# The first stage takes v ahead of q and k, and layer 0's output path goes ahead of the exponentials

## The chip, the cores and the metric

The kernel runs on one core of a Trainium2 chip. The metric is the time of one execution on the device, in microseconds (us). The five engines of the core are TensorE (PE, with its weight loads as PEld), VectorE (DVE), ScalarE (ACT), GpSimd (POOL) and SyncE (SP), whose queue starts the large transfers.

## The reference, cut to what matters

A decoder trunk of two layers on 256 positions of width 1024. Layer 0 mixes with differential attention, layer 1 with block attention, which for 256 positions is causal attention with 16 heads. Each mixer is followed by a squared-ReLU MLP of width 4096.

```python
h = x
for i in range(2):
    hn = rmsnorm(h, attn_norm[i])
    m = diff_attention(...) if i == 0 else moba_attention(...)
    h = h + m
    h = h + squared_relu_mlp(rmsnorm(h, mlp_norm[i]), w_ff1[i], w_ff2[i])
return rmsnorm(h, final_norm)

# diff_attention: q, k, v = split(hn @ w_in); two score maps p[0], p[1] per head, 8 heads
lam = exp(sum(lf[0] * lf[1])) - exp(sum(lf[2] * lf[3])) + lam_init
a = p[0] - lam * p[1]
o = rmsnorm(a @ v, subln_w) * (1 - lam_init)     # per head
return o @ w_out
```

## The kernel before

**Precision and weights.** Every weight product is made in three matmuls. A weight tile `raw` is split into `hi`, its rounded value (ScalarE, line 141), and `lo`, the rest (VectorE, line 142), and the activations are split in the same way into a high and a low half. `raw` tiles are loaded in units of 1 MB (128 x 2048 floats). Four `raw` buffers and five pairs `hi`/`lo` rotate, so a load waits until the unit four places earlier is split. The list `units` sets the order of the loads. For layer 0 it is: q and k of head 0, the two halves of v's first 512 columns, q and k of heads 1 to 4, v's second half, the other heads, `w_out`, the MLP.

**The first stage** is `start()` and the first block of `mixer(0)`. It stands under `tc.manual_schedule()`, in which the instructions made inside keep the written order on each engine. TensorE first transposes the identity `WARM` times, then the gains, then x: 16 transposes into seven banks of PSUM, first the eight of the first 128 positions, then those of the others. `x_out` (line 214) writes a slice of x, transposed and scaled by the gain, as a high half (ScalarE) and a low half (VectorE). Between the slices stand the splits of unit 0 and then unit 1, in pieces of 512 columns, two of them with `lo` on GpSimd. Then come the sums of squares of x's second half, `root_r` (1/rms, on GpSimd), head 0's q and k (`qk`, 48 matmuls of 256 columns), the first half of `v` (24 matmuls of 512 columns), the split of unit 2, `scale_r` (which writes R, the row factor of q and k), `qk_out` (head 0's q and k times R), the splits of units 3 and 4 and the second half of `v`.

`load_gains()` and `load_lambda()` stand behind that block. There the planner of the framework sets the order on all engines but TensorE, by priorities and by its own estimate of durations, and it may put an instruction ahead of or between those of the block. `tc.high_priority(offset=n)` moves an instruction n places forward in priority (SOONER = 100); split_until uses a negative one (LATER = 150).

**Behind it** TensorE's order is written out and kept (lines 515 to 598): the matmuls of head h, and between them `scores` (with `soft`: the reductions on VectorE and exponentials on ScalarE), `a2` (transposes of the weights of attention to `aT`), `a3` (the product with v, its norm: squares on ScalarE, `on` on VectorE), `a4` (transposes to `oT`, written by `o_out` on ScalarE and VectorE) and `wo` (the products with `w_out`, three matmuls each).

Of the kernel before, what the change touches and what calls it, by code (L numbers as in the profile page):

```python
# [9 lines left out]
F32 = mybir.dt.float32  # L10
F32R = mybir.dt.float32r
# [13 lines left out]
RING = 2048  # L25
LOOK = 3
PIECE = 1024
WARM = 12
LATER = 150
SOONER = 100  # L30

# [2 lines left out]
def kernel(  # L34
# [45 lines left out]
    for i in range(2):  # L80
        qkv = w_in[i].rearrange("(kc d) c -> d kc c", d=P)
        wo = w_out[i].rearrange("(h e) d -> e h d", e=P)
        f1 = w_ff1[i].rearrange("(kc d) f -> d kc f", d=P)
        f2 = w_ff2[i].rearrange("(f p) d -> p f d", p=P)

        def qk_unit(h):
            U[i, "qk", h] = unit([P, 2, KC, P], [
                ((slice(None), s, slice(a, a + n)), qkv[:, a:a + n, s * D + h * P: s * D + (h + 1) * P])
                for s in range(2) for n in ((KC, 4)[i == 0 and h == 0],) for a in range(0, KC, n)])

        def v_unit(g):
            for a in range(2):
                U[i, "v", g, a] = unit([P, 4, 512], [
                    ((slice(None),), qkv[:, 4 * a:4 * a + 4, 2 * D + g * 512: 2 * D + (g + 1) * 512])])

        qk_unit(0)
        v_unit(0)
        for h in range(1, 5):
            qk_unit(h)
        v_unit(1)  # L100
        for h in range(5, 8):
# [13 lines left out]

        for a in range(2):
            f1_unit(0, a)
        for j in range(1, 8):
            for a in range(2):
                f1_unit(j, a)  # L120
                f2_unit(j - 1, a)
        for a in range(2):
            f2_unit(7, a)
# [8 lines left out]
            nc.sync.dma_start(raw[where], src)  # L132
        d["raw"] = raw

    def split_piece(u, c, n, eng=nc.vector):
# [4 lines left out]
        r, h, l = (d[k].rearrange(letters(d["shape"]))[:, c:c + n] for k in ("raw", "hi", "lo"))  # L140
        nc.scalar.activation(h, r, AF.Copy)  # L141
        eng.tensor_tensor(l, r, h.bitcast(F32), op=ALU.subtract)  # L142

    state = dict(loaded=0, done=0, ahead=0)

# [48 lines left out]

    nlam = const.tile([P, 1], F32, name="nlam")

    def load_lambda():
        both = work.tile([1, 4, HD], F32, tag="on", name="lampr", bufs=3)
        pr, one = both[:, 0:2], both[:, 2:4].rearrange("p a b -> p (a b)")
        sm = const.tile([1, 4], F32, name="lamsm")  # L200
        nc.vector.memset(one, 1.0)
        nc.vector.tensor_tensor(pr, lamt[:, 0::2], lamt[:, 1::2], op=ALU.mult)
        nc.vector.reduce_sum(sm[:, 0:2], pr, axis=mybir.AxisListType.X)
        nc.scalar.activation(sm[:, 2:4], sm[:, 0:2], AF.Exp)
        nc.vector.tensor_tensor(sm[:, 0:1], sm[:, 3:4], sm[:, 2:3], op=ALU.subtract)
        nc.vector.tensor_scalar(sm[:, 0:1], sm[:, 0:1], lam_init, None, op0=ALU.subtract)
        t = ps("tp", "lamps")
        mm(t[:, :1], one, sm[:, 0:1], start=True, stop=True)
        nc.vector.tensor_copy(nlam, t[:, :1])


# [42 lines left out]
        return r  # L254


    def start():
        nc.sync.dma_start(xs[:, 0], x_v[:, 0])
        nc.scalar.dma_start(grow0, attn_norm[0].rearrange("(a b) -> a b", b=P))
        nc.sync.dma_start(xs[:, 1], x_v[:, 1])  # L260
        load_until(4)
        load_small()
        load_until(6)
        warm = const.tile([P, 2], F32, name="warm")
        nc.vector.memset(warm, 0.0)
# [7 lines left out]
        parts = new_parts("x")
        xt = xT[0, "a"] = work.tile([P, KC, 2 * T], F32R, tag="xT", name="xT_0a", bufs=1)
        x_ps = [ps(tag, f"xtp0_{j}", bufs) for j, (tag, bufs) in
                enumerate([("acc", 4)] * 4 + [("tp", 2)] * 2 + [("mm", 2)])]
        x_ps = [t_ps[:, :T] for t_ps in x_ps] + [x_ps[4][:, T:]]
        for t in range(NT):
            for kc in range(KC):
                nc.tensor.transpose(x_ps[kc][:, t * P:(t + 1) * P], xs[:, t, kc * P:(kc + 1) * P], ident)  # L280
        for n in range(2):
            sumsq("x", 0, n, parts)
        for kc in range(KC):
            x_out(xt, kc, x_ps[kc], kc)
            if kc in (0, 3):
                split_piece(0, kc // 3 * 512, 512)
            if kc == 6:
                split_piece(0, 1024, 512, nc.gpsimd)
        split_piece(0, 1536, 512, nc.gpsimd)
        for c in range(0, RING, 512):  # L290
            split_piece(1, c, 512)
        state["done"] = 2
        for n in range(2):
            sumsq("x", 1, n, parts)
        return parts
# [4 lines left out]
    def mixer(i, parts):  # L300
# [14 lines left out]
        def qk(h, s, k0, k1, out=True):  # L315

            hi, lo = need(i, "qk", h)
            if s == 0 and k0 == 0:
# [7 lines left out]
            if s == 1 and k1 == KC and out:  # L326
                qk_out(h)

        def qk_out(h):
            o = work.tile([P, 2 * T], F32, tag="qk", name=f"qk{i}_{h}", bufs=4)  # L330
# [3 lines left out]

        def v(g, a):
            hi, lo = need(i, "v", g, a)
            if a == 0:
                S["vp", g] = [ps("acc", f"v{i}_{g}_{t}", 4) for t in range(NT)]
            for t in range(NT):
                o = S["vp", g][t]  # L340
                for c in range(4):
                    kc = 4 * a + c
                    xh, xl = (xt[:, kc, b + t * P: b + (t + 1) * P] for b in (0, T))
                    mm(o, xh, hi[:, c], start=kc == 0, stop=False)  # L344
                    mm(o, xh, lo[:, c], start=False, stop=False)  # L345
                    mm(o, xl, hi[:, c], start=False, stop=kc == KC - 1)  # L346
                if a == 1:
                    vs = work.tile([P, 512], F32, tag="vs", name=f"vs{i}_{g}_{t}", bufs=4)
                    nc.scalar.activation(vs, o, AF.Copy, scale=S["r"][:, t:t + 1])
                    S["v", g, t] = vs  # L350
# [109 lines left out]
        def a4(h):  # L460
            if i == 1:
                return
            t_ps = ps("tp", f"ot{i}_{h}")
            for t in range(NT):
                nc.tensor.transpose(t_ps[:, t * P:(t + 1) * P], S["on", h][:, t], ident)
            o_out(h, t_ps[:, :T], gT[:, GS:])

        def wo(n, t, *hs):
            if ("wo", n, t) not in S:
# [329 lines left out]
```

## Time and profile before

| | |
|---|---|
| median of 3 runs | 605.03 us (604.67 to 605.85) |
| the profiled execution | 604.88 us |
| its span, first to last instruction | 603.1 us |
| TensorE busy | 591.5 us (98%) |
| VectorE, ScalarE, GpSimd busy | 379.8, 318.7, 55.1 us |
| granted TensorE clock, mean | 0.996 |
| read from HBM | 102.25 MB |

In the rows below, a timeline row gives the start and the duration in us, the engine, the line, the operation, what is written and read, and the count of instructions that were merged; in brackets stands the idle time of the engine just before and what ended it. Matmuls overlap, so the distance of two starts, not the duration, is what one costs. Line numbers are those of the kernel before.

### The profile page before, as it was taken

The page shows a single profiled execution, that of the slowest core. Times are in us where ns is not written, and L with a number is a line of the kernel's source. Part 1 is how long each engine was busy: PE and PEld are TensorE (multiplying, and loading weights), DVE is VectorE, ACT ScalarE, POOL GpSimd, SP SyncE. Part 2 cuts the span into 40 slices and gives each one's busy share as a digit, 9 for nine tenths or more (in the row PEclk, how much of TensorE's full clock was granted, in tenths as well). Part 3 has the DMA queues.
Part 4 walks back from the last instruction along what each step waited for, and adds up shares of the span by engine and source line. Part 5 has one row for each costly group of instructions (what it writes and reads, how often), then busy time and mean ns, then how long its engine had stood idle before and what let it go on. Part 6 is the DMA issues. An engine that isn't in the chain of part 4 may idle for free.

```text
span 603.1 us, 8781 instructions
## 1 busy us (share of the span) xinstructions
PE 591.5 (98%) x3368; PEld 506.2 (84%) x3368; DVE 379.8 (63%) x704; ACT 318.7 (53%) x614; POOL 55.1 (9%) x82
## 2 busy tenths in 40 slices
PE   7999999999999999999999999999999999999995
PEld 6899897888888888888889988878888888888884
DVE  4798578488466466466566664638776476476534
ACT  5776476375354354354474656637554454454413
POOL 5001011000000000000000661500000000000003
PEclk8999999999999999999999999999999999999999
DMA  9996444166646646646848436533566646645001
GB/s 303 264 329 222 148 132 140 71 210 200 211 148 204 214 141 210 209 140 199 215 145 210 141 139 180 174 102 108 182 203 213 201 143 218 199 140 209 0 1 70
DMA packets 85258, 103.87 MB, mean 172 GB/s; under 512 B 2112, under 2 KB 67936, under 8 KB 85216
## 3 DMA queue, kind: packets, MB, share of 16 engines
q1 hardware_dynamic: 84896, 103.03, 54.8%
q8 instruction: 26, 0.43, 0.3%
q10 hardware_dynamic: 160, 0.27, 0.1%
q14 instruction: 16, 0.13, 0.1%
q0 software_dynamic: 160, 0.01, 0.0%
HBM read 102.25 MB, written 1.05 MB: 171 GB/s over the span
## 4 chain that ended last, share of the span: by engine, by line
PE 92%; DVE 2%; ACT 2%; POOL 1%; DMA 1%; issue 1%; POOLq 0%; DVEq 0%
PE y L644 29%; PE f L620 20%; PE f L621 10%; PE z L323 5%; PE z L324 5%; PE z L325 5%; PE v L345 2%; PE v L346 2%; PE v L344 2%; PE wo L478 2%; PE wo L480 2%; PE wo L479 2%; PE s L363 2%; PE at L410 1%; ACT e L386 1%; PE o L433 1%
## 5 line engine op out<-in xcount | busy, mean ns | idle before, releaser
L142 DVE TENSOR_TENSOR lo<-raw,hi 128x1024 fp32r<-128x1024 f32 (+1 forms) x194 | 232.5, 1211 | 130.4 <-ACT hi L141 130.1
L141 ACT ACTIVATE hi<-raw 128x1024 fp32r<-128x1024 f32 (+1 forms) x196 | 197.5, 1038 | 150.5 <-PE f L620 84.6
L644 PE MATMUL y<-hi,h 128*128 128x512 f32 x504 | 167.7, 396 | 0.0
L644 PEld LDWEIGHTS y<-hi,h 128*128 128x128 f32 x504 | 94.8, 188 | 23.1 <-ACT h L629 0.3
L644 PE MATMUL y<-lo,h 128*128 128x512 f32 x252 | 99.9, 397 | 0.0
L620 PE MATMUL f<-xT_(1, 'm')_4142,hi 128*128 128x512 f32 x256 | 91.9, 397 | 0.0
L620 PE MATMUL f<-xT_(0, 'm')_1443,hi 128*128 128x512 f32 x256 | 91.9, 397 | 0.0
L621 PE MATMUL f<-xT_(1, 'm')_4142,lo 128*128 128x256 f32 x256 | 72.3, 282 | 0.0
L621 PE MATMUL f<-xT_(0, 'm')_1443,lo 128*128 128x256 f32 x256 | 72.3, 282 | 0.0
L620 PEld LDWEIGHTS f<-xT_(0, 'm')_1443,hi 128*128 128x128 f32 x256 | 48.2, 188 | 11.7
L620 PEld LDWEIGHTS f<-xT_(1, 'm')_4142,hi 128*128 128x128 f32 x256 | 48.2, 188 | 11.7
L644 PEld LDWEIGHTS y<-lo,h 128*128 128x128 f32 x252 | 47.4, 188 | 8.9
L629 ACT ACTIVATE h<-zs 128x256 fp32r<-128x256 f32 x64 | 26.0, 410 | 46.2 <-DVE zs L627 46.2
L621 PEld LDWEIGHTS f<-xT_(1, 'm')_4142,lo 128*128 128x128 f32 x256 | 48.1, 188 | 1.2
L621 PEld LDWEIGHTS f<-xT_(0, 'm')_1443,lo 128*128 128x128 f32 x256 | 48.1, 188 | 1.2
L325 PE MATMUL z<-xT_0a,lo 128*128 128x256 f32 x128 | 36.4, 285 | 2.3 <-DVE lo L142 2.3
L323 PE MATMUL z<-xT_0a,hi 128*128 128x256 f32 x128 | 37.6, 293 | 0.0
L323 PE MATMUL z<-xT_(1, 'a')_2915,hi 128*128 128x256 f32 x128 | 36.7, 286 | 0.0
L324 PE MATMUL z<-xT_0a,hi 128*128 128x256 f32 x128 | 36.6, 286 | 0.0
L630 DVE TENSOR_TENSOR h<-zs,h 128x256 fp32r<-128x256 f32 x64 | 27.0, 424 | 15.0 <-ACT h L629 14.5
L625 ACT ACTIVATE zs<-f 128x256 f32<-128x256 f32 x64 | 23.9, 375 | 23.4 <-PE f L621 23.4
L324 PE MATMUL z<-xT_(1, 'a')_2915,hi 128*128 128x256 f32 x128 | 35.9, 280 | 0.0
(190 smaller groups left out, 826.6 us busy)
## 6 DMA issues: line engine op xcount, KB each, us to landing
raw<-in_w_ff_dram SPq DMA_DIRECT2D x64, 1024.0 KB, 5.4
raw<-in_w_in_dram SPq DMA_DIRECT2D x30, 512.0 KB, 5.6
raw<-in_w_in_dram SPq DMA_DIRECT2D x8, 1024.0 KB, 5.1
raw<-in_w_out_dram SPq DMA_DIRECT2D x8, 1024.0 KB, 5.2
xs<-in_x_dram SPq DMA_DIRECT2D x2, 512.0 KB, 3.9
raw<-in_w_in_dram SPq DMA_DIRECT2D x4, 256.0 KB, 5.5
fg<-in_final_norm_dram SPq DMA_DIRECT2D x2, 256.0 KB, 3.9
out_dram<-xg SPq DMA_DIRECT2D x2, 256.0 KB, 2.0
```

Source lines behind the costliest of these rows:

```text
L141: nc.scalar.activation(h, r, AF.Copy)
L142: eng.tensor_tensor(l, r, h.bitcast(F32), op=ALU.subtract)
L323: mm(z, hi[:, s, kc], xh, start=s == 0 and kc == 0, stop=False, skip_group_check=True)
L324: mm(z, hi[:, s, kc], xl, start=False, stop=False, skip_group_check=True)
L325: mm(z, lo[:, s, kc], xh, start=False, stop=s == 1 and kc == KC - 1, skip_group_check=True)
L344: mm(o, xh, hi[:, c], start=kc == 0, stop=False)
L620: mm(z, hi[:, kc, c], xt[:, kc], start=kc == 0, stop=False, skip_group_check=True)
L621: mm(z[:, :T], lo[:, kc, c], xt[:, kc, :T], start=False, stop=kc == KC - 1, skip_group_check=True)
L625: nc.scalar.activation(zs, z[:, T:], AF.Copy)
L629: nc.scalar.activation(h[:, :T], zs, AF.Copy)
L630: nc.vector.tensor_tensor(h[:, T:], zs, h[:, :T].bitcast(F32), op=ALU.subtract)
L644: mm(acc[n, t], a, w[:, f % 2, n * 512:(n + 1) * 512], start=f == 0 and w is hi and a is hh, skip_group_check=i == 1, stop=a is hl and (f ...
```

## The change

In the first stage v's first half becomes unit 0 and 1, ahead of head 0's q and k (now unit 2). x is loaded in two halves of its columns (all positions each) instead of two halves of its positions, with the first two slices of unit 0 between them. x is transposed two slices at a time into one bank (`x_slice`), and v's matmuls of a slice follow as soon as it is split; slices 4 to 7 follow in pairs, with the split of unit 1 in pieces of 1024 columns. No `lo` goes to GpSimd any more. All four sums of squares stand behind x. `load_gains` and the two parts of the lambda work stand in the written order inside the block. The split of unit 3 (head 1) stands at its end, and unit 4 behind it. Outside the first stage, `a3` of layer 0 and the `o_out` of heads 4 and 5 get SOONER. WARM goes from 12 to 10.

```diff
-WARM = 12
+WARM = 10
 ...
+        if i == 0:
+            v_unit(0)
         qk_unit(0)
-        v_unit(0)
+        if i == 1:
+            v_unit(0)
 ...
-    def load_lambda():
-        both = work.tile([1, 4, HD], F32, tag="on", name="lampr", bufs=3)
 ...
+    def lambda_sums():
+        nc.vector.memset(lam_ab[:, 2:4], 1.0)
+        nc.vector.tensor_tensor(lam_ab[:, 0:2], lamt[:, 0::2], lamt[:, 1::2], op=ALU.mult)
+        nc.vector.reduce_sum(lam_s[:, 0:2], lam_ab[:, 0:2], axis=mybir.AxisListType.X)
+
+    def lambda_out():
+        nc.scalar.activation(lam_s[:, 2:4], lam_s[:, 0:2], AF.Exp)
+        nc.vector.tensor_tensor(lam_s[:, 0:1], lam_s[:, 3:4], lam_s[:, 2:3], op=ALU.subtract)
+        nc.vector.tensor_scalar(lam_s[:, 0:1], lam_s[:, 0:1], lam_init, None, op0=ALU.subtract)
         t = ps("tp", "lamps")
+        mm(t[:, :1], lam_ab[:, 2:4].rearrange("p a b -> p (a b)"), lam_s[:, 0:1], start=True, stop=True)
         nc.vector.tensor_copy(nlam, t[:, :1])
 ...
+    def start_loads():
         nc.scalar.dma_start(grow0, attn_norm[0].rearrange("(a b) -> a b", b=P))
 ...
+        nc.sync.dma_start(xs[:, :, :512], x_v[:, :, :512])
+        for c in range(2):
+            nc.sync.dma_start(u["raw"][:, c:c + 1], src[:, c:c + 1])
+        nc.sync.dma_start(xs[:, :, 512:], x_v[:, :, 512:])
+        nc.sync.dma_start(u["raw"][:, 2:], src[:, 2:])
+        state["loaded"] = 1
+        load_until(6)
         load_small()
-        load_until(6)
 ...
+    def x_slice(g):
+        t_ps = ps("tp", f"xtp0_{g}")
+        for c in range(2):
+            for t in range(NT):
+                nc.tensor.transpose(t_ps[:, c * T + t * P: c * T + (t + 1) * P],
+                                    xs[:, t, (2 * g + c) * P:(2 * g + c + 1) * P], ident)
+        return [t_ps[:, c * T:(c + 1) * T] for c in range(2)]
 ...
         def a3(*hs):
+            with tc.high_priority(offset=SOONER if i == 0 else 0):
+                a3_(*hs)
 ...
-            o_out(h, t_ps[:, :T], gT[:, GS:])
+            with tc.high_priority(offset=SOONER if h in (4, 5) else 0):
+                o_out(h, t_ps[:, :T], gT[:, GS:])
 ...
             with tc.manual_schedule():
-                parts = start()
+                start_loads()
+                start_warm()
+                parts = new_parts("x")
+                xt = xT[0, "a"] = work.tile([P, KC, 2 * T], F32R, tag="xT", name="xT_0a", bufs=1)
+                xp = x_slice(0) + x_slice(1)
+                for kc in range(4):
+                    x_out(xt, kc, xp[kc], kc)
+                    split_piece(0, kc * 512, 512)
+                    v_mm(0, [(t, kc) for t in range(NT)], units[0]["hi"], units[0]["lo"])
+                    if kc >= 2:
+                        xp += x_slice(kc)
+                for kc in range(4, 8, 2):
+                    x_out(xt, kc, xp[kc], kc)
+                    x_out(xt, kc + 1, xp[kc + 1], kc + 1)
+                    split_piece(1, (kc - 4) * 512, 1024)
+                v_mm(0, [(t, kc) for kc in range(4, 8) for t in range(NT)], units[1]["hi"], units[1]["lo"])
+                for n in range(2):
+                    for t in range(NT):
+                        sumsq("x", t, n, parts)
+                lambda_sums()
                 root_r()
-                xt = xT[i, "a"]
-                qk(0, 0, 0, 8, out=False)
-                qk(0, 1, 0, 8, out=False)
-                v(0, 0)
+                state["done"] = 2
                 split_until(3)
+                qk_mm(0, 0, 0, 8, units[2]["hi"], units[2]["lo"])
+                load_gains()
                 scale_r()
+                qk_mm(0, 1, 0, 8, units[2]["hi"], units[2]["lo"])
+                lambda_out()
+                v_out(0)
                 qk_out(0)
-                split_until(5)
-                v(0, 1)
+                split_until(4)
             state["ahead"] = LOOK
-            load_gains()
-            load_lambda()
```

`qk_mm`, `v_mm` and `v_out` are the matmuls of `qk`, those of `v` and the copies at the end of `v` as functions of their own. In `v_mm` the three matmuls of a slice and a half of the positions follow one another: x high with `hi`, x high with `lo`, x low with `hi`.

## Rows read from the trace of the kernel before

**Rows 1.** The page, part 1: busy time, share of the span and count by engine.
```profile
PE 591.5 (98%) x3368; PEld 506.2 (84%) x3368; DVE 379.8 (63%) x704; ACT 318.7 (53%) x614; POOL 55.1 (9%) x82
```
**Rows 2.** Waits of TensorE, whole span: us in total, times, longest.
```profile
PE z L325 <- DVE lo L142: 2.3, 1, 2.3
...
PE wo L478 <- ACT oT L421: 0.9, 1, 0.9
PE at L410 <- DVE on L457: 0.2, 1, 0.2
```
**Rows 3.** Timeline of TensorE, 4.5 to 14.1 us.
```profile
4.50 3.34 PE L280 MATMUL xtp<-ident,xs 128*128 128x128 f32 x16
...
5.19 1.06 PE L280 MATMUL xtp<-ident,xs 128*128 128x128 f32 x4
...
7.11 0.73 PE L280 MATMUL xtp<-ident,xs 128*128 128x128 f32 x4
7.76 0.38 PE L323 MATMUL z<-xT_0a,hi 128*128 128x256 f32 x1
7.99 0.28 PE L324 MATMUL z<-xT_0a,hi 128*128 128x256 f32 x1
10.58 0.44 PE L325 MATMUL z<-xT_0a,lo 128*128 128x256 f32 x1 [2.32 <-DVE lo L142]
...
14.09 0.33 PE L324 MATMUL z<-xT_0a,hi 128*128 128x256 f32 x1
```
**Rows 4.** Timeline of VectorE, first 31 us.
```profile
9.64 0.28 DVE L202 TENSOR_TENSOR lampr<-lamt 1x128 f32<-1x128 f32 x1 [1.94 <-DMA lamt<-in_diff_lambda_dram]
9.85 0.67 DVE L142 TENSOR_TENSOR lo<-raw,hi 128x512 fp32r<-128x512 f32 x1
10.46 1.25 DVE L217 SCALAR_TENSOR_TENSOR xT_0a<-xtp,gT,xT_0a 128x256 fp32r<-128x256 f32 x3
...
24.63 0.69 DVE L332 TENSOR_TENSOR qk<-z,R 128x512 f32<-128x512 f32 x1 [3.57 <-ACT R L313]
25.57 4.63 DVE L142 TENSOR_TENSOR lo<-raw,hi 128x1024 fp32r<-128x1024 f32 x4 [0.26 <-ACT hi L141]
```
**Rows 5.** Windows: stretch, length, busy (instructions) by engine, granted clock, DMA share, GB/s.
```profile
10.75:11.00 0.25, 0.25 (x2) 0.21 (x3) 0.25 (x2) 0.19 (x1) 0.00 (x0) 0.55 1.07 401
14.00:14.25 0.25, 0.25 (x3) 0.25 (x2) 0.25 (x2) 0.25 (x2) 0.00 (x0) 0.63 1.10 342
18.00:23.00 5.00, 5.00 (x23) 4.03 (x22) 2.79 (x6) 1.61 (x2) 0.73 (x1) 1.00 1.21 295
30.00:38.00 8.00, 8.00 (x69) 8.00 (x69) 8.00 (x12) 7.22 (x8) 0.00 (x0) 1.00 1.09 359
```
**Rows 6.** The page, part 6: DMA issues, KB each, us from issue to landing.
```profile
xs<-in_x_dram SPq DMA_DIRECT2D x2, 512.0 KB, 3.9
```
**Rows 7.** Timeline of ScalarE, first 29 us.
```profile
6.72 0.47 ACT L216 ACTIVATE xT_0a<-xtp,gT 128x256 fp32r<-128x256 f32 x1 [1.05 <-PE xtp L280]
7.09 0.62 ACT L141 ACTIVATE hi<-raw 128x512 fp32r<-128x512 f32 x1
...
23.93 0.39 ACT L312 ACTIVATE R<-rps 128x256 f32<-128x256 f32 x1 [4.32 <-PE rps L311]
...
24.48 3.90 ACT L141 ACTIVATE hi<-raw 128x1024 fp32r<-128x1024 f32 x4
```
**Rows 8.** Timeline of TensorE, 97 to 106 us.
```profile
97.68 0.39 PE L465 MATMUL ot<-ident,on 128*128 128x128 f32 x2
...
105.31 0.83 PE L445 MATMUL o<-vs,aT 128*128 128x128 f32 x6
```
**Rows 9.** Timeline of ScalarE, 101 to 105 us.
```profile
101.52 0.82 ACT L421 ACTIVATE oT<-ot,gT 128x256 fp32r<-128x256 f32 x2
102.23 2.00 ACT L141 ACTIVATE hi<-raw 128x1024 fp32r<-128x1024 f32 x2
104.13 0.49 ACT L412 ACTIVATE aT<-at 128x384 f32<-128x384 f32 x1
```

More of the change, by code (lines that the diff above doesn't have):

```diff
@@ L88, in qk_unit @@
                 ((slice(None), s, slice(a, a + n)), qkv[:, a:a + n, s * D + h * P: s * D + (h + 1) * P])
-                for s in range(2) for n in ((KC, 4)[i == 0 and h == 0],) for a in range(0, KC, n)])
+                for s in range(2) for a, n in ((0, KC),)])
         def v_unit(g):
@@ L133, in load, with split_tiles @@
         d["raw"] = raw
-    def split_piece(u, c, n, eng=nc.vector):
+    def split_tiles(u):
         d = units[u]
@@ L139, in split_piece, with split_part @@
             d["lo"] = wsp.tile(d["shape"], F32R, tag="lo", name=f"lo{u}")
-        r, h, l = (d[k].rearrange(letters(d["shape"]))[:, c:c + n] for k in ("raw", "hi", "lo"))
+        return d["raw"], d["hi"], d["lo"]
+    def split_part(r, h, l):
         nc.scalar.activation(h, r, AF.Copy)
-        eng.tensor_tensor(l, r, h.bitcast(F32), op=ALU.subtract)
+        nc.vector.tensor_tensor(l, r, h.bitcast(F32), op=ALU.subtract)
+    def split_piece(u, c, n):
+        split_part(*(k.rearrange(letters(units[u]["shape"]))[:, c:c + n] for k in split_tiles(u)))
     state = dict(loaded=0, done=0, ahead=0)
@@ L195 @@
     nlam = const.tile([P, 1], F32, name="nlam")
-    def load_lambda():
-        both = work.tile([1, 4, HD], F32, tag="on", name="lampr", bufs=3)
[L199 to L206, printed above, removed]
+    lam_ab = work.tile([1, 4, HD], F32, tag="on", name="lampr", bufs=3)
+    lam_s = const.tile([1, 4], F32, name="lamsm")
+    def lambda_sums():
[6 more added lines that the diff above has]
+        nc.vector.tensor_scalar(lam_s[:, 0:1], lam_s[:, 0:1], lam_init, None, op0=ALU.subtract)
         t = ps("tp", "lamps")
-        mm(t[:, :1], one, sm[:, 0:1], start=True, stop=True)
+        mm(t[:, :1], lam_ab[:, 2:4].rearrange("p a b -> p (a b)"), lam_s[:, 0:1], start=True, stop=True)
         nc.vector.tensor_copy(nlam, t[:, :1])
@@ L254, in rsqrt, with start_warm @@
         return r
-    def start():
-        nc.sync.dma_start(xs[:, 0], x_v[:, 0])
+    def start_loads():
         nc.scalar.dma_start(grow0, attn_norm[0].rearrange("(a b) -> a b", b=P))
-        nc.sync.dma_start(xs[:, 1], x_v[:, 1])
-        load_until(4)
+        u = units[0]
+        u["raw"] = wraw.tile(u["shape"], F32, tag="raw", name="raw0")
+        src = u["pieces"][0][1]
+        nc.sync.dma_start(xs[:, :, :512], x_v[:, :, :512])
[5 more added lines that the diff above has]
+        load_until(6)
         load_small()
-        load_until(6)
+    def start_warm():
         warm = const.tile([P, 2], F32, name="warm")
@@ L272, in start @@
         nc.vector.tensor_copy(gT[:, :KC], t_ps[:, P:P + KC])
[L273 to L295, printed above, removed]
+    def x_slice(g):
[5 more added lines that the diff above has]
+        return [t_ps[:, c * T:(c + 1) * T] for c in range(2)]
     slopes8 = [2.0 ** (-8.0 * (h + 1) / 8) for h in range(8)]
@@ L317, in qk, with qk_mm @@
             hi, lo = need(i, "qk", h)
+            qk_mm(h, s, k0, k1, hi, lo)
+            if s == 1 and k1 == KC and out:
+                qk_out(h)
+        def qk_mm(h, s, k0, k1, hi, lo):
             if s == 0 and k0 == 0:
@@ L325, in qk @@
                 mm(z, lo[:, s, kc], xh, start=False, stop=s == 1 and kc == KC - 1, skip_group_check=True)
-            if s == 1 and k1 == KC and out:
-                qk_out(h)
         def qk_out(h):
@@ L336, in v, with v_mm, v_out @@
             hi, lo = need(i, "v", g, a)
-            if a == 0:
-                S["vp", g] = [ps("acc", f"v{i}_{g}_{t}", 4) for t in range(NT)]
-            for t in range(NT):
[L340 to L350, printed above, removed]
+            v_mm(g, [(t, 4 * a + c) for t in range(NT) for c in range(4)], hi, lo)
+            if a == 1:
+                v_out(g)
+        def v_mm(g, tk, hi, lo):
+            if (0, 0) in tk:
+                S["vp", g] = [ps("acc", f"v{i}_{g}_{t}", 4) for t in range(NT)]
+            for t, kc in tk:
+                o = S["vp", g][t]
+                c = kc % 4
+                xh, xl = (xt[:, kc, b + t * P: b + (t + 1) * P] for b in (0, T))
+                mm(o, xh, hi[:, c], start=kc == 0, stop=False)
+                mm(o, xh, lo[:, c], start=False, stop=False)
+                mm(o, xl, hi[:, c], start=False, stop=kc == KC - 1)
+        def v_out(g):
+            for t in range(NT):
+                vs = work.tile([P, 512], F32, tag="vs", name=f"vs{i}_{g}_{t}", bufs=4)
+                nc.scalar.activation(vs, S["vp", g][t], AF.Copy, scale=S["r"][:, t:t + 1])
+                S["v", g, t] = vs
         blocks = ((0, slice(0, P)), (1, slice(P, 384)))
@@ L426, in a3, with a3_ @@
         def a3(*hs):
+            with tc.high_priority(offset=SOONER if i == 0 else 0):
+                a3_(*hs)
+        def a3_(*hs):
             O = {h: ps("tp", f"o{i}_{h}") for h in hs}
```

## The prediction

> **What bounds the kernel now.** I read the page first. TensorE is busy for 591.5 us of a span of 603.1, 98% [rows 1], so the time is the sum of its instructions plus its few waits and whatever stretch runs at the low clock. The waits of TensorE come next. Behind its first instruction it has only three: 2.3 us for a `lo` tile of the weights, 0.9 us for an `oT` tile and 0.2 us for a buffer that `on` frees [rows 2]. So only two places can gain: the first 15 us and the output path of layer 0 near 100 us. The profiled execution took 604.88 us, 1.78 more than its span. The sum below is made against 604.88. The median of the other runs, 605.03, lies 0.15 above it.
>
> The timeline shows the start. Sixteen transposes of x run from 4.50 to 7.76, about 0.21 us apart. Two matmuls on q weights follow, and then nothing starts until 10.58 [rows 3]. VectorE shows why. It stood at a lambda instruction for 1.94 us until the DMA of lambda landed at 9.64, and the `lo` tile that TensorE wanted was queued behind it [rows 4]. The clock comes after that. The granted clock is half (1.2 of 2.4 GHz) from about 10.8 to 14.2, right behind the empty stretch [rows 5]. The granted column shows full speed before that, but the instructions say otherwise. Four transposes took 1.06 us around 5.2 and 0.73 us from 7.11 on [rows 3], so the engine was slow until about 7.2.
>
> **The change, part by part.** *Removed at the start.* From the matmul at 7.99 to the one at 10.58 the list has 2.59 us where 0.12 is normal (69 matmuls in 8 us [rows 5]), so 2.47 goes. From 10.58 to 14.09, 14 matmuls on 256 columns take 3.51 us [rows 3] where 14 x 0.118 = 1.65 would do, so 1.86 goes, if the clock stays up. Lambda now stands behind the sums of squares, and its DMA has long landed by then, so it costs nothing. Eight of the 16 transposes of x move to about 12 us, to full speed: 8 x (0.21 - 0.11) = 0.8. Together 5.1 us.
>
> *Added at the start.* The loads of x by columns move the same bytes. The old halves took 3.9 us to land [rows 6], the first new one stands first on the queue too, and I keep 4.3 for it. The pieces of v behind it, 256 KB each, are due about 0.7 us after one another at the 342 to 401 GB/s of [rows 5], ahead of their use. Two warm-up transposes less end in time that TensorE waits anyway. So only four waits are to be priced.
>
> (a) The first matmul. Eight transposes end at 4.5 + 8 x 0.21 = 6.2. The first bank of four is done at about 5.65. ScalarE then takes 0.37 for `x_out` until the split can start, and 0.62 for the split [rows 7], so the first matmul starts at 6.65. The second needs `lo`, 0.67 more on VectorE [rows 4], and starts at 7.4. TensorE stands for 0.45 + 0.45 = 0.9. Bounds: 0.5, if `x_out` need not wait for the whole bank, and 1.6, if the first transfer lands 0.7 later. After that each slice of x costs VectorE 0.42 + 0.67 = 1.1 and TensorE six matmuls of 0.23 (23 in 5 us [rows 5]) = 1.4, so the vector engines keep ahead for slices 0 to 3.
>
> (b) The second half of v. Slices 4 and 5 are transposed behind slice 2's matmuls. From there the chain is two `x_out`s (0.75), a split of 1024 columns on ScalarE (3.90 / 4 = 0.98 [rows 7], 1.05 for one alone), VectorE's half of it (4.63 / 4 = 1.16 [rows 4]) and 0.2 of hand-overs, about 3.1. TensorE meanwhile has slice 3 (1.4) and four transposes (0.4). It waits 1.25. Bounds 0.6 and 1.7, by how far the engines overlap.
>
> (c) Head 0's weights are split after four sums of squares on ScalarE. By the same durations they arrive 0.2 after TensorE (bounds 0 and 0.6).
>
> (d) Head 1's weights. In the first stage each engine keeps the written order. The trace shows it: ScalarE stood for 4.32 us before R, and the splits behind it, with all their data there, followed only at 24.48 [rows 7]; VectorE did the same before `qk_out` [rows 4]. The change puts the split of head 1 last, behind `lambda_out`, `v_out` and `qk_out`. VectorE can start `qk_out` only when head 0's last matmul and the lambda matmul are through, about 0.45 later. It takes 0.6 to hand over and the `lo` half 1.2, so it is ready 2.3 after the matmuls of head 0. TensorE is at that matmul after 0.55 and waits 1.75. Before, 5.6 us of v matmuls covered this split; now nothing does. Bounds 0.8 (if `qk_out` overlaps further) and 2.4. Behind the waiting matmul stands all of TensorE's list.
>
> Together 0.9 + 1.25 + 0.2 + 1.75 = 4.1.
>
> (e) The clock. It was up at about 7.2, after transposes without a break from 4.50. Now that run ends at 6.2, with two gaps behind it. If it rises at the same time all the same, the cost is 0. If it comes as late behind the first steady matmuls as it did in the slow stretch, 3.4 us [rows 5], it is up at 10.8, and half of 3.4 us is lost: 1.7. The work from 7.4 on is like the work in that stretch, so I take a value nearer that end, 1.2.
>
> The Trainium skill, TensorE: Matmul & The Clock Gate, section Part 4: PE-mode transpose, says that transposes do not raise the clock, since they don't count as busy in the way that matmuls do. This trace disagrees: the transposes sped up before any weight matmul had run [rows 3]. By that rule term (e) would be the full 1.7 and the time half a microsecond more than I forecast; that is rival 4.
>
> Net at the start: -5.1 + 4.1 + 1.2 = +0.2.
>
> *The output path of layer 0.* The transposes of head 4 are done at about 98.1 [rows 8], but ScalarE wrote its `oT` only at 101.52, behind all exponentials of heads 6 and 7 [rows 9]. With the two tiles put 100 places sooner that wait ends: -0.94. The 0.2 us wait for `on` should go with the raised `a3`: -0.19. What is late next: the exponentials move back by the two tiles (0.7), so ScalarE's work up to 102.23 and the two splits behind it end when they did, and `aT` of head 6 is still written at 104.13 [rows 9]. TensorE wants it at 105.31 - 0.94 = 104.37 [rows 8], and it is complete at 104.62: +0.25 (bounds 0, if it comes ahead of a split, and 0.5). Together -0.9 (bounds -1.1 and 0).
>
> Everything after that is TensorE's own list, with no wait in the trace. The splits run later than before: those of head 2 were done at 30.2 [rows 4] and are now due near 32.7, and TensorE comes to them after head 1's 48 matmuls, near 35. That cover is 2 us, and I cost them at 0.
>
> *Sum:* +0.2 - 0.9 = -0.7, so 604.88 - 0.7 = 604.2 for the profiled execution, 604.3 beside the median.
>
> **Rivals.**
> 1. *The clock is up early and the waits overlap more.* For it: the transposes did raise it in the trace, and half as many stand there again. Against it: their run is broken. (e) goes to 0 and (b) or (d) to 0.2 less: 604.3 - 1.4 = 602.9.
> 2. *Slower: the wait before head 1 drops the clock.* TensorE stands still for 1.75 us at about 27 us. The empty 2.3 us of rows 2 were followed by the half clock; the 0.9 us at 102 were not. [...] The price is what the trace shows for such a stretch, 1.86, and where the clock is that easily lost, (e) is at its upper end (0.5 more): 604.3 + 2.4 = 606.7.
> 3. *The output path does not move.* The order outside the first stage is made by the planner, and a raised priority helps only where the planner believes the tile ready. Then the 0.9 stays: 605.2.
> 4. *Transposes don't count for the clock.* Then the clock rises only behind the weight matmuls, at 10.8 (1.7 instead of 1.2): 604.8. The quicker transposes from 7.11 on [rows 3] speak against it.
>
> **How the numbers follow.** The forecast, 604.3, has 0.34 and its own range is 603.6 to 605.2. Rival 1 has 0.32, rival 2 has 0.16, rival 3 has 0.10, rival 4 has 0.08. A change under 0.2%, 1.2 us, can hardly be told from none here. Below 603.8 lie nearly all of rival 1 and a sixth of the forecast: 0.37 for faster. Above 606.2 lie most of rival 2 and a little of rival 3: 0.14. The rest, 0.49, is no change. The range goes from 602.5 (rival 1 with two waits at their lower bounds) to 606.4 (rival 2 with (e) at its middle value).
>
> **What would show it.** The trace after should have no wait for the DMA of lambda. TensorE's first weight matmul should stand near 6.7 and the second near 7.4, with a wait of about 1.2 near 14 us and one of 1.75 before `z` of head 1, near 28 us. The chain from x should be read by the spacing of the v matmuls: 0.43 apart until the clock is up, 0.23 after. The `oT` rows of heads 4 and 5 should stand among the exponentials. I am wrong if `z` of head 1 doesn't wait, if the clock is full from the first v matmul on, or if a wait of over 1 us shows up behind 40 us.

## The result: 7 us slower, half of it at the start and half behind it

The changed kernel takes 611.97 us (611.81 to 614.38), the kernel before 604.93 on the same chip: a ratio of 1.0123 (95% interval 1.0096 to 1.015). I had forecast 604.3, from 602.5 to 606.4. The profiled execution took 611.91 us, 7.03 more than that of before.

First, how much work there is. Part 1 of the page of the changed kernel:

```profile
PE 592.5 (97%) x3366; PEld 504.6 (83%) x3366; DVE 379.9 (62%) x704; ACT 318.7 (52%) x612; POOL 52.5 (9%) x80
```

TensorE is busy 1.0 us longer than in [rows 1], in a span 7.0 us longer. So the loss is nearly all waiting. Two places in the timelines say where it arose: the start of the scores of heads 0 and 1 on TensorE, and the first sum of a `w_out` product on VectorE. Start and duration in us, before:

```profile
38.48 1.58 PE L363 MATMUL s<-qk 64*128 64x128 f32 x16
...
116.73 1.39 DVE L486 TENSOR_TENSOR xs<-wo,xs 128x512 f32<-128x512 f32 x2 [3.93 <-PE wo L480]
```

and after:

```profile
42.22 1.58 PE L375 MATMUL s<-qk 64*128 64x128 f32 x16
...
123.80 1.39 DVE L503 TENSOR_TENSOR xs<-wo,xs 128x512 f32<-128x512 f32 x2 [3.93 <-PE wo L497]
```

The scores start 3.74 us later, where I had forecast +0.2. From the scores to the `w_out` sum (I call it stretch 2) it takes 81.58 us instead of 78.25, that is +3.33, where I had forecast -0.9. Together 7.07. Behind it the two kernels take the same time: 603.1 - 116.73 = 486.4 and 610.1 - 123.80 = 486.3.

The waits of TensorE after (us in total, times, longest):

```profile
PE ot L481 <- DVE oT L434: 4.1, 2, 2.3
PE z L333 <- DVE lo L147: 2.3, 2, 1.5
...
PE xtp L296 <- DMA xs<-in_x_dram: 1.2, 1, 1.2
PE wo L497 <- DVE oT L434: 0.2, 1, 0.2
```

The wait on an `oT` tile of [rows 2] fell from 0.9 to 0.2. The first row is new and the largest, and I had not named it. The timeline of TensorE after, with the idle time before an instruction and what ended it in brackets:

```profile
1.55 2.39 PE L288 MATMUL wps<-ident 128*128 128x128 f32 x10 [1.55 <-POOL ident masks.py:199]
...
5.37 1.97 PE L296 MATMUL xtp<-ident,xs 128*128 128x128 f32 x8 [1.22 <-DMA xs<-in_x_dram]
7.56 0.79 PE L354 MATMUL v<-hi,xT_0a 128*128 128x512 f32 x1 [0.23 <-ACT hi L146]
8.29 0.79 PE L355 MATMUL v<-lo,xT_0a 128*128 128x512 f32 x1
...
11.86 0.40 PE L354 MATMUL v<-hi,xT_0a 128*128 128x512 f32 x1
...
17.09 0.49 PE L354 MATMUL v<-hi,xT_0a 128*128 128x512 f32 x1 [0.70 <-ACT hi L146]
...
18.35 0.50 PE L355 MATMUL v<-lo,xT_0a 128*128 128x512 f32 x1 [0.77 <-DVE lo L147]
...
24.27 0.28 PE L332 MATMUL z<-xT_0a,hi 128*128 128x256 f32 x1
25.28 0.38 PE L333 MATMUL z<-xT_0a,lo 128*128 128x256 f32 x1 [0.74 <-DVE lo L147]
...
31.95 0.28 PE L332 MATMUL z<-xT_0a,hi 128*128 128x256 f32 x1
33.78 0.38 PE L333 MATMUL z<-xT_0a,lo 128*128 128x256 f32 x1 [1.55 <-DVE lo L147]
...
67.30 0.44 PE L481 MATMUL ot<-ident,on 128*128 128x128 f32 x2 [2.29 <-DVE oT L434]
...
95.96 0.44 PE L481 MATMUL ot<-ident,on 128*128 128x128 f32 x2 [1.78 <-DVE oT L434]
```

The forecast waits are there, with one more: two at the first matmuls, two instead of one in v's second half (17.09 and 18.35), one before head 0 (25.28), longer than forecast, and 1.55 before head 1 (33.78). The two at 67.30 and 95.96 stand before the `ot` transposes of heads 1 and 3.

### The profile page after: what moved, and what is told of

Its sections match the earlier page's. It is cut to its first block, busy times and chain, and to the rows that moved or that the text cites. A ratio compares the mean times of both kernels' runs of the same rounds, so it can differ in the third digit from the quotient of the medians.

```text
span 610.1 us, 8769 instructions
## 1 busy us (share of the span) xinstructions
PE 592.5 (97%) x3366; PEld 504.6 (83%) x3366; DVE 379.9 (62%) x704; ACT 318.7 (52%) x612; POOL 52.5 (9%) x80
## 4 chain that ended last, share of the span: by engine, by line
PE 85%; DVE 7%; ACT 3%; DMA 2%; issue 1%; POOL 1%; POOLq 0%; DVEq 0%
PE y L679 28%; PE f L655 20%; PE f L656 10%; PE z L331 3%; DVE lo L147 3%; PE z L333 3%; PE z L332 3%; PE v L354 2%; PE v L355 2%; PE wo L495 2%; PE wo L497 2%; PE v L356 2%; PE wo L496 2%; ACT hi L146 1%; PE s L375 1%
## 5 line engine op out<-in xcount | busy, mean ns | idle before, releaser
L655 PE MATMUL f<-xT_(0, 'm')_1434,hi 128*128 128x512 f32 x256 | 91.9, 397 | 0.0
L655 PE MATMUL f<-xT_(1, 'm')_4133,hi 128*128 128x512 f32 x256 | 91.9, 397 | 0.0
L656 PE MATMUL f<-xT_(1, 'm')_4133,lo 128*128 128x256 f32 x256 | 72.3, 282 | 0.0
L656 PE MATMUL f<-xT_(0, 'm')_1434,lo 128*128 128x256 f32 x256 | 72.3, 282 | 0.0
L655 PEld LDWEIGHTS f<-xT_(1, 'm')_4133,hi 128*128 128x128 f32 x256 | 48.2, 188 | 11.7
L655 PEld LDWEIGHTS f<-xT_(0, 'm')_1434,hi 128*128 128x128 f32 x256 | 48.2, 188 | 11.7
L656 PEld LDWEIGHTS f<-xT_(1, 'm')_4133,lo 128*128 128x128 f32 x256 | 48.1, 188 | 1.2
L656 PEld LDWEIGHTS f<-xT_(0, 'm')_1434,lo 128*128 128x128 f32 x256 | 48.1, 188 | 1.2
L331 PE MATMUL z<-xT_0a,hi 128*128 128x256 f32 x128 | 36.8, 287 | 0.0
L331 PE MATMUL z<-xT_(1, 'a')_2906,hi 128*128 128x256 f32 x128 | 36.7, 286 | 0.0
L332 PE MATMUL z<-xT_(1, 'a')_2906,hi 128*128 128x256 f32 x128 | 35.9, 280 | 0.0
```

Source lines behind the costliest of these rows:

```text
L655: mm(z, hi[:, kc, c], xt[:, kc], start=kc == 0, stop=False, skip_group_check=True)
L656: mm(z[:, :T], lo[:, kc, c], xt[:, kc, :T], start=False, stop=kc == KC - 1, skip_group_check=True)
```

## The experiments

Each ratio is to runs of the kernel before on the same chip; those had medians from 605.26 to 605.69. The time is the median of the runs. "Scores" and "stretch 2" are the two measures from above; they are read from the one profiled execution of each kernel.

| kernel | time | ratio [95%] | scores | stretch 2 |
|---|---|---|---|---|
| before | 604.93 to 605.69 | 1 | 38.48 | 78.25 |
| after | 611.97 | 1.0123 [1.0096, 1.015] | 42.22 | 81.58 |
| a_noprio | 610.06 | 1.0073 [1.0058, 1.0088] | 43.07 | 79.02 |
| a_noa3 | 609.4 | 1.006 [1.0046, 1.0073] | 43.10 | 78.49 |
| a_oout_all | 612.68 | 1.012 [1.0099, 1.0142] | 43.01 | 83.12 |
| b_a3 | 608.53 | 1.0053 [1.0036, 1.0069] | 38.62 | 81.20 |
| b_oout | 604.23 | 0.9982 [0.9973, 0.9991] | 38.56 | 77.66 |
| a_head1 | 609.73 | 1.0067 [1.0052, 1.0082] | 40.97 | 80.51 |
| a_banks | 611.32 | 1.0097 [1.0081, 1.0114] | 39.65 | 83.38 |
| a_warm | 611.83 | 1.0107 [1.0084, 1.013] | 42.53 | 83.11 |
| a_xcols | 612.62 | 1.0119 [1.0101, 1.0137] | 42.94 | 81.56 |
| b_lam | 602.75 | 0.9955 [0.994, 0.997] | 35.92 | 79.01 |
| b_lam_oout | 602.31 | 0.9951 [0.9936, 0.9966] | 35.78 | 77.78 |
| a_fixed | 603.2 | 0.9961 [0.9948, 0.9973] | 37.25 | 77.76 |

**Stretch 2: which of the two priorities?** The theory: the raised `a3` makes the new `ot` waits. The rival: raising only two of the eight `oT` tiles does it. Four kernels, two from either side.

b_a3, the kernel before with only `a3` raised:
```diff
 def a3(*hs):
+    with tc.high_priority(offset=SOONER if i == 0 else 0):
+        a3_(*hs)
```


> The kernel before with a3 of layer 0 raised by 100 places and nothing else. Theory 1: the ot transposes wait twice for about 2 us, in heads 1 and 3, so 604.9 + 4 = about 609. Theory 2: no such wait, 604.7 to 604.9.

Measured 608.53, scores unmoved and stretch 2 longer by 2.95. Its waits of TensorE hold the two of the changed kernel, at the same heads; the first is 1.21 here instead of 2.29, the second 1.78 as there:
```profile
PE ot L469 <- DVE oT L422: 3.0, 2, 1.8
...
PE wo L482 <- ACT oT L421: 0.9, 1, 0.9
```
```profile
62.84 0.44 PE L469 MATMUL ot<-ident,on 128*128 128x128 f32 x2 [1.21 <-DVE oT L422]
```
The `wo` row shows that `a3` alone does not bring `oT` of head 4 forward either.

b_oout, the kernel before with only the `o_out` of heads 4 and 5 raised:
```diff
-            o_out(h, t_ps[:, :T], gT[:, GS:])
+            with tc.high_priority(offset=SOONER if h in (4, 5) else 0):
+                o_out(h, t_ps[:, :T], gT[:, GS:])
```


> The kernel before with o_out of heads 4 and 5 raised and nothing else. Both theories: the 0.9 us wait before wo goes and nothing comes for it, 604.9 - 0.9 = 604.0. If the planner is not moved by it, 604.9.

Measured 604.23. Stretch 2 is 0.59 shorter, and the wait at `wo` is down to 0.2. This half of the output path is a small gain, as forecast.

a_noprio, the changed kernel with neither raised:
```diff
-offset=SOONER if i == 0 else 0
+offset=0
 ...
-offset=SOONER if h in (4, 5) else 0
+offset=0
```


> The changed kernel with both priorities of the output path taken back (a3 and o_out as before), the first stage as changed. Theory 1: the two new waits of the ot transposes (2.3 and 1.8 us) come from the raised a3. Then they vanish, the 0.9 us wait before wo comes back, and the time is 612.0 - 4.1 + 0.9 = 608.8. Theory 2 (rival): they come from the first stage, which ends 3.7 us later and makes the planner choose another order. Then they stay and the time is about 612.9.

Measured 610.06. The `ot` waits are gone and stretch 2 is 79.02. That is still 0.77 above before, by two waits of TensorE for `on` (0.8 together) that before had once with 0.2 [rows 2]. The new one:
```profile
66.17 0.55 PE L422 MATMUL at<-ident,e 128*128 128x128 f32 x3 [0.64 <-DVE on L473]
```
The time is 1.3 above theory 1, by this wait and by scores that came 0.85 later than in the changed kernel (the clock, below).

a_oout_all, the changed kernel with the `oT` tiles of all eight heads raised:
```diff
-offset=SOONER if h in (4, 5) else 0
+offset=SOONER
```


> The changed kernel with o_out of all heads of layer 0 raised, not only of heads 4 and 5. If the new waits of ot come from this, that a3 was raised past the oT of heads 0 and 2, which stayed where they were, they go and the time is 612.0 - 4.1 = 607.9. If raising a3 delays the oT tiles in another way (its squares among the exponentials), they stay at 2 us each: 612.

Measured 612.68. The rival falls: the `ot` waits are still 3.9 us. In the profiled execution, the slowest of the four, TensorE also stood at the half clock behind the first of them (68 to 72 us, below).

a_noa3, the changed kernel with only `a3` not raised:
```diff
-offset=SOONER if i == 0 else 0
+offset=0
```


> The changed kernel with only the raised a3 taken back; o_out of heads 4 and 5 stays raised. Theory: the two waits of ot (4.1 us) are all that the raised a3 brought, and o_out of heads 4 and 5 alone removes the wait before wo: 612.0 - 4.1 + 0.2 (the wait for on comes back) = 608.1, and what is left over the kernel before, 2.7 to 3, is the first stage (3.7) less the output path (0.9). Rival: the raised a3 also helped somewhere (the norms of heads 4 to 7 come sooner), and taking it back gains under 3 us.

Measured 609.4. Stretch 2 is 3.09 shorter than in the changed kernel. The time fell by 2.6 only, because in its profile the scores came 0.9 later (the clock, below).

How the raised `a3` does it stands in the order on VectorE. After, 62 to 67 us:
```profile
62.37 0.15 DVE L470 SCALAR_TENSOR_TENSOR v<-sq,c 128x2 f32<-128x2 f32 x1
...
63.40 0.61 DVE L473 TENSOR_SCALAR on<-o,rs_o 128x128 f32<-128x128 f32 x2 [0.72 <-POOL rs_o L263]
...
64.64 0.68 DVE L338 TENSOR_TENSOR qk<-z,R 128x512 f32<-128x512 f32 x1
...
65.63 1.22 DVE L147 TENSOR_TENSOR lo<-raw,hi 128x1024 fp32r<-128x1024 f32 x1
66.77 0.48 DVE L434 SCALAR_TENSOR_TENSOR oT<-ot,gT,oT 128x256 fp32r<-128x256 f32 x1
```
Before, the same work at 59 to 62 us:
```profile
59.03 0.15 DVE L454 SCALAR_TENSOR_TENSOR v<-sq,c 128x2 f32<-128x2 f32 x1
59.10 0.68 DVE L332 TENSOR_TENSOR qk<-z,R 128x512 f32<-128x512 f32 x1
60.07 0.61 DVE L457 TENSOR_SCALAR on<-o,rs_o 128x128 f32<-128x128 f32 x2 [0.28 <-POOL rs_o L253]
60.60 0.47 DVE L422 SCALAR_TENSOR_TENSOR oT<-ot,gT,oT 128x256 fp32r<-128x256 f32 x1
60.99 1.22 DVE L142 TENSOR_TENSOR lo<-raw,hi 128x1024 fp32r<-128x1024 f32 x1
```
The reader is to see two things. Before, `qk_out` fills the time in which GpSimd works out `rs_o`, and `oT` of head 0 follows `on` directly, ahead of the split. After, `on` was raised, so VectorE comes to it sooner and stands still for 0.72; `qk_out` and a split of 1.22 then come ahead of `oT`. The same order stands at the second wait (`on` at 92.06 after 0.60 of standing, the split at 94.29, `oT` at 95.42). The first of these `oT` frees the bank of PSUM that `ot` of head 1 needs, and TensorE waits 2.29 for it. Without the raise, in a_noa3, the old order is back:
```profile
65.57 0.61 DVE L473 TENSOR_SCALAR on<-o,rs_o 128x128 f32<-128x128 f32 x2 [0.28 <-POOL rs_o L263]
66.09 0.48 DVE L434 SCALAR_TENSOR_TENSOR oT<-ot,gT,oT 128x256 fp32r<-128x256 f32 x1
```

**The start: the wait before head 1.** a_head1, the changed kernel with the split of head 1 directly behind that of head 0, ahead of R, lambda and `qk_out`:
```diff
                 state["done"] = 2
-                split_until(3)
+                split_until(4)
 ...
-                split_until(4)
```


> The changed kernel with head 1's split (unit 3) moved up, directly behind head 0's, ahead of lambda_out, v_out and qk_out. Theory (step d of the prediction): the wait of 1.7 us at the lo matmul of head 1 comes only from that place in the written order, since ScalarE and VectorE stand idle for 3.8 and 2 us before; it goes, and the scores of heads 0 and 1 start 1.6 to 1.8 us sooner than at 42.2. Rival: the data of unit 3 are late too (transfer or splits), and the wait moves by less than half a microsecond.

Measured 609.73; the wait before head 1 is gone:
```profile
PE ot L481 <- DVE oT L434: 3.0, 2, 1.8
...
PE z L333 <- DVE lo L147: 0.8, 1, 0.8
```
The 0.8 left is head 0's. Scores came 1.25 sooner, not 1.6 to 1.8, with a clock that rose later (near 13 us; 11.9 in the changed kernel). Stretch 2 is 1.07 shorter too, since the first `ot` wait is down from 2.29 to the 1.21 of b_a3:
```profile
64.98 0.44 PE L481 MATMUL ot<-ident,on 128*128 128x128 f32 x2 [1.21 <-DVE oT L434]
```
So the late split of head 1 costs a second time, some 30 us behind its own wait. The other changed kernels agree. Those that keep the wait before head 1 have a first `ot` wait of 2.06 to 2.36 or, without the raised `a3`, the new wait for `on` of a_noprio (0.64; 0.66 in a_noa3). a_fixed, without either, has only the 0.2 for `on` of the kernel before. By which steps the late split does this was not followed.

**The start: the shared bank.** In the changed kernel slices 4 and 5 of x lie in one bank. ScalarE's `x_out` of slice 5 stood behind VectorE's of slice 4, though the two slices lie in different halves of it:
```profile
14.59 0.47 ACT L226 ACTIVATE xT_0a<-xtp,gT 128x256 fp32r<-128x256 f32 x1 [3.41 <-PE xtp L296]
15.62 0.47 ACT L226 ACTIVATE xT_0a<-xtp,gT 128x256 fp32r<-128x256 f32 x1 [0.55 <-DVE xT_0a L227]
...
18.72 0.48 ACT L226 ACTIVATE xT_0a<-xtp,gT 128x256 fp32r<-128x256 f32 x1 [1.32 <-DVE xT_0a L227]
```
The last row is slice 7 behind slice 6. ScalarE stood for 1.32 there, since VectorE came to slice 6 only behind a split of 1024 columns.

a_banks puts neighbours in different banks:
```diff
-                    if kc >= 2:
-                        xp += x_slice(kc)
+                    if kc == 2:
+                        xp += x_pairs()   # slices 4, 6 in one bank, 5, 7 in the other
```


> The changed kernel with slices 4 to 7 of x transposed together behind slice 2's matmuls into two banks so that slices 4 and 6 share one and 5 and 7 the other. Theory: in the changed kernel ScalarE's x_out of slice 5 waits for VectorE's of slice 4, because both slices lie in one bank (0.55 us idle, twice); in two banks it does not, and slice 6 is there earlier too. The two waits at the first matmuls of v's second half (0.94 and 1.03) shrink by about 0.6 in all. Rival: the order is set by something else than the bank (the write to xT), the 0.55 stays, and nothing is gained.

Both stalls went: the two `x_out`s of each pair follow one another. From the first transpose of slice 4 (13.46; 13.95 in the changed kernel) to the first `lo` matmul of v's second half (17.41; 18.35) it takes 3.95 us instead of 4.40.
```profile
14.31 0.84 ACT L226 ACTIVATE xT_0a<-xtp_p,gT 128x256 fp32r<-128x256 f32 x2 [2.84 <-PE xtp_p L306]
```
Head 0's wait went too: its first two `z` matmuls stand 0.11 apart, at 23.00 and 23.11. Scores came 2.57 sooner. These two, and 0.3 more in v's second half, make 1.7 (0.45 + 0.9 + 0.3). In this profile the clock rose at about 10.7, 1.1 sooner than in the changed kernel, which gives half of that, 0.5. Another 0.3 lies behind the wait before head 1: the matmuls of head 1 stand 0.113 us apart here (31.73 to 39.44) and 0.118 in the changed kernel (34.00 to 42.01), for a reason that the traces do not show. The whole gained only 0.65, because behind an `ot` wait of 2.36 TensorE fell to the half clock (64 to 68 us, mean granted 0.66).

**The start: the clock.** a_warm, the changed kernel with WARM = 17, so that transposes run without a break until x has landed:
```diff
-WARM = 10
+WARM = 17
```


> The changed kernel with WARM = 17 instead of 10, so that TensorE transposes without a break until x has landed (1.55 to about 5.2). Theory: the clock came late (11.6 to 13.9 us in three runs of this first stage) because TensorE stood still from 4.1 to 5.3 and issued only eight transposes behind that; with the gap filled it is up by about 8, the v matmuls are 0.23 apart from then on, and the scores start 1.5 us sooner than at 42.2. Rival: transposes do not raise the clock; it comes 3 to 4 us behind the first weight matmul as before, and nothing changes.

Its timeline of TensorE:
```profile
1.55 3.89 PE L288 MATMUL wps<-ident 128*128 128x128 f32 x17 [1.55 <-POOL ident masks.py:199]
...
8.74 0.39 PE L356 MATMUL v<-hi,xT_0a 128*128 128x512 f32 x1
8.97 0.40 PE L354 MATMUL v<-hi,xT_0a 128*128 128x512 f32 x1
...
32.56 0.39 PE L333 MATMUL z<-xT_0a,lo 128*128 128x256 f32 x1 [1.55 <-DVE lo L147]
```
The v matmuls are 0.23 apart almost from the first; the eight from the second on take 1.96 us (8.41 to 10.37), where in the changed kernel they took 3.57 (8.29 to 11.86), 0.45 each. Only transposes had run before 7.6 us. That goes against the Trainium skill, TensorE: Matmul & The Clock Gate, section Part 4: PE-mode transpose, by which transposes don't count. Yet the median gained nothing (611.83). The profiled execution, with 613.75 the slowest of the four (the fastest took 610.95), lost the clock twice again: behind the wait before head 1, and behind the `ot` wait of 2.06 at 67.60 (granted 0.60 from 68 to 72 us). Its stretch 2, 83.11, is 1.5 longer than that of the changed kernel. A window behind the first (length, busy by engine, granted clock, DMA share, GB/s):
```profile
35.00:36.00 1.00, 1.00 (x7) 1.00 (x6) 1.00 (x2) 1.00 (x3) 0.00 (x0) 0.50 0.54 147
```
The changed kernel, with the same wait of 1.55, kept it:
```profile
34.00:38.00 4.00, 4.00 (x35) 4.00 (x35) 4.00 (x4) 4.00 (x5) 0.00 (x0) 1.00 0.50 126
```

**The start: the landing of x.** The first half of x lands 4.6 us after its issue, the first of before after 3.4. a_xcols puts both halves ahead of the pieces of v on the queue, to tell the shape of the transfer (rows of 2 KB, two per partition, instead of 4 KB) from what is queued behind it:
```diff
+        nc.sync.dma_start(xs[:, :, 512:], x_v[:, :, 512:])
         for c in range(2):
             nc.sync.dma_start(u["raw"][:, c:c + 1], src[:, c:c + 1])
-        nc.sync.dma_start(xs[:, :, 512:], x_v[:, :, 512:])
```


> The changed kernel with both column halves of x ahead of the three pieces of v on the queue. The first half landed 4.6 us after its issue, the first half by positions of the kernel before 3.4. Theory: the pieces of v queued right behind share the engines with it; with x's second half behind it instead it is the same amount of work in flight, so it stays at about 4.6 and the cause is the shape of the transfer (two rows of 2 KB a partition instead of one of 4 KB). Rival: it is the pieces of v, and the first half lands at 3.4 and the transposes start at 4.3 instead of 5.3, 1 us sooner.

The transposes start at 4.96, between the 4.50 of [rows 3] and the 5.37 after: of the 0.87, 0.41 goes with the order and 0.46 stays with the shape. In the five other profiles with the changed kernel's order and WARM = 10 they start between 5.19 and 5.38, so this division is good to some 0.2. Nothing is gained, since v's pieces now come late and the first v matmul starts at 7.87 instead of 7.56. The first row of its TensorE:
```profile
4.96 1.97 PE L296 MATMUL xtp<-ident,xs 128*128 128x128 f32 x8 [0.82 <-DMA xs<-in_x_dram]
```

**One part alone.** b_lam, the kernel before with lambda and the gains in the written order at the end of the first block, and nothing else:
```diff
+                load_gains()
+                load_lambda()
             state["ahead"] = LOOK
-            load_gains()
-            load_lambda()
```


> The kernel before with load_gains and load_lambda moved into the written order, behind v's second half at the end of the first block, and nothing else. Theory: the first wait (2.3 us) is the one of VectorE for the DMA of lambda; without it lo is ready at about 8.5 and the clock does not fall either: 2.1 + 1.5 less, about 601.5. Rival: the next thing in line (VectorE's low halves of x, with GpSimd's lo pieces behind) takes most of it back, and less than 1.5 us is gained.

Measured 602.75. The empty stretch of [rows 3] and the half clock of [rows 5] are both gone, and scores start 2.56 sooner. That shows what I had read from before: lambda's DMA held up VectorE, and the clock fell for that reason. The gain is less than the 4.33 that the forecast had for the two (2.47 + 1.86). In this kernel the next in line hold TensorE up instead: low halves of x (0.4), `hi` (0.2) and `lo` (0.2). Stretch 2 gave back 0.76. The one new wait there is 0.31 for `e` at 43.66; the rest was not found.

b_lam_oout is b_lam with the two raised `o_out` of b_oout.

> The kernel before with only two parts: the lambda work in the written order, and o_out of heads 4 and 5 raised. Each gained by itself (602.75 against 605.66, 604.23 against 605.43). Theory: they lie in different places of TensorE's list and add up: 605.6 - 2.9 - 1.2 = 601.5. Rival: the planner chooses another order behind the earlier start and one of them is lost: about 602.8.

Measured 602.31, the lowest median of all. The interval overlaps that of b_lam, so the times do not show that the two gains add up. Its profile has no wait of TensorE over 0.4 behind the first instruction, and its stretch 2, 77.78, has none of the 0.76 of b_lam.

a_fixed is the changed kernel without the raised `a3`, and with the edits of a_head1, a_banks and a_warm.

> The changed kernel without the raised a3, with head 1's split moved up, slices 4 to 7 in two banks and WARM = 17; v still goes ahead of q and k. By the single runs the first stage gets shorter by 1.5 (head 1), 1.5 (banks, with the wait at head 0 that went along) and 1.5 to 2.5 (clock), and the waits of ot (4.1) go: 612 - 9 = 603, so v first would gain 2 us over the kernel before. Rival: the parts cover each other (the vector engines are the limit once the clock is up early), and it comes out no better than the kernel before, 605.

Measured 603.2. So a kernel with v ahead of q and k can be faster than before. It has lambda's new place and the raised `o_out` of b_lam_oout as well, and it is not shown to be better or worse than that one, whose interval overlaps; so no gain is shown from v's place itself. What it still waits for is v's own chain:
```profile
PE v L365 <- DVE lo L147: 1.0, 2, 0.8
PE v L364 <- ACT hi L146: 0.8, 2, 0.5
```

## Why the prediction was wrong

**What was right.** *Removed:* the wait for lambda and the half clock behind it are gone in the changed kernel, and b_lam shows that lambda's place does it. The eight transposes that moved to full speed take 2 x 0.36 = 0.72 (0.88 by my figure of 0.11). *(a):* from the first transpose to the first matmul 2.19 (forecast 2.15), to the second 0.73 (0.75). *(d):* 33.78 - 31.95 less the normal 0.12 is 1.71 (1.75), and a_head1 takes the wait away. *The two `oT` tiles:* they came ahead of exponentials and the 0.9 became 0.2, worth 0.59 in b_oout where I had 0.69 (-0.94 + 0.25). The 0.25 is not where I had put it: TensorE has no wait for `aT` of head 6, and 0.2 stays at `wo` itself.

**The step that failed most: "What is late next", asked of the raised `a3` in one place only.** I took its raise for a gain of 0.19 at `on` near 100 us. But it moves `a3` of all heads of layer 0, and I did not follow VectorE's order past heads 0 and 2. There it costs 2.95 to 3.09 (b_a3 and a_noa3). Stretch 2 missed the forecast by 4.2 us. The raised `a3` is 3.1 of it: +2.95 in b_a3, where I had -0.19. The `oT` tiles are 0.1: 0.59 in b_oout, where I had 0.69. The last 1.0 appears only with the changed start. It is the first `ot` wait, 2.29 instead of 1.21, and a_head1 shows that it comes from the late split of head 1. So term (d) was right at its own place and had a second price further down. I had put that at nothing: of the later splits I looked only at TensorE's own matmuls of head 2 ("I cost them at 0"). The prediction named a wait of over 1 us behind 40 us as a sign that it is wrong; there are two, 2.29 and 1.78.

**The start, 3.54 above the forecast.** By the terms of the sum, (b) to (d) as distances of starts less the normal distance:

| term | forecast | measured | more by |
|---|---|---|---|
| x lands later | 0 | 5.37 - 4.50 = 0.87 | 0.87 |
| (a) first two matmuls | 0.9 | as forecast | 0.0 |
| (b) second half of v | 1.25 | 0.94 + 1.03 + 0.2 | 0.9 |
| (c) head 0 | 0.2 | 25.28 - 24.27 - 0.12 = 0.89 | 0.7 |
| (d) head 1 | 1.75 | 1.71 | 0.0 |
| (e) the clock | 1.2 | 3.57 - 8 x 0.233 = 1.71 | 0.5 |
| the rest, not singled out | 0 | some 0.6 | 0.6 |

I had x's delay only as an upper bound of (a), 0.7, and forecast nothing; the trace of before had no transfer of that shape. Term (b) lacked the stalls on the shared bank (0.45 + 0.3 in a_banks), and (c) followed from (b): it went with it. Term (e) rested on a misreading. I had the clock of before rise "after transposes without a break from 4.50", but the row of before goes back to 1.55:
```profile
1.55 2.82 PE L270 MATMUL wps<-ident 128*128 128x128 f32 x12 [1.55 <-POOL ident masks.py:199]
```
These twelve end where the transposes of x begin. With ten, and x landing later, TensorE stood for 1.22 ahead of them, and the clock rose only at 11.9. I had put the two warm-up transposes at nothing; a_warm, which fills the gap, has the full clock from the third v matmul on (8.74). The rest is the difference to 3.54; part of it is that the first matmul behind each wait or change of shape stands some 0.1 longer (0.34 from 18.35 to the next, against 0.23).

**The rivals.** Rival 1 is refuted: (b) was larger and the clock came later. Rival 2, the slower one, had the right sign, but its mechanism was not what made this kernel slower: behind the 1.55 at 33.78, and behind 2.29 at 67.30, the clock stayed full (granted 1.00), while in a_warm it fell behind 1.55. The length of the wait alone does not decide. Rival 3 is refuted by the `wo` row. Rival 4 has the right price for (e), 1.7, by chance: a_warm shows that transposes do raise the clock, and with seven more of them in place of the break the same eight matmuls are 1.6 faster (3.57 - 1.96).

**What stays open.** The clock rose at 11.9 in the changed kernel's profile, at 13.8 to 13.9 in those of a_noprio, a_noa3 and a_oout_all, and at 10.7 in a_banks, with nearly the same start. Waits of 1.5 to 2.4 us were followed by half clock in some profiles and not in others. What decides was not found. Why a_oout_all still has its `ot` waits is not settled either: ScalarE's part of `oT` of head 0 is written at 64.61 there, but VectorE's part comes at 67.55, behind the same `qk_out` and split as in the changed kernel, though it was raised.

## What to carry to other kernels

Before raising the priority of work on an engine that keeps its order, follow each of its instructions to what it waits for on another engine: VectorE standing 0.7 us for GpSimd put 1.2 us on TensorE three steps on, and 2.3 behind the later start. Do it for each repetition of the code, not only for the place that the edit is meant for. And when one wait is the trouble, take away that wait first: putting lambda where its data had landed (b_lam, 602.75) was worth as much as the best form of the larger change that was run (a_fixed, 603.2).

## What the runs showed that I had not expected

- The granted clock can read 1.00 where TensorE runs at half speed. In the changed kernel the v matmuls start 0.43 us apart from 8.88 to 11.02, and 0.23 from 11.86 on; the window in between (columns as above) shows nothing of it, so at the start the clock must be read from the spacing:

```profile
10.00:11.00 1.00, 1.00 (x3) 0.73 (x3) 0.67 (x2) 1.00 (x3) 0.00 (x0) 1.00 1.06 413
```

- Two engines that read different halves of one bank of PSUM took turns: ScalarE stood for VectorE for 0.55 and 1.32 us in the changed kernel, and not at all with the halves in two banks (a_banks). Whether the chip or the software keeps them apart, no run here shows.
- A wait can cost a second time: in a_oout_all the clock fell behind an `ot` wait of 2.08 us, and the window right behind it has 20 matmuls in 4 us at a granted clock of 0.57. In the changed kernel, behind the 2.29 at the same place, the window has 29 at 1.00, and stretch 2 is 1.5 shorter. First a_oout_all, then the changed kernel:

```profile
68.00:72.00 4.00, 3.91 (x20) 3.92 (x21) 1.62 (x3) 0.47 (x1) 0.00 (x0) 0.57 0.35 106
```
```profile
68.00:72.00 4.00, 4.00 (x29) 3.72 (x29) 1.88 (x4) 1.76 (x3) 0.00 (x0) 1.00 0.64 175
```
